# Decay rows of the delta net and mLSTM: spread over the partitions by DMA instead of by matmul

## The chip, the cores and the metric

The kernel runs on one core of a Trainium2 chip. The metric is the device time of one execution in microseconds (us). The engines are TensorE (PE; its weight loads are PEld), VectorE (DVE), ScalarE (ACT), GpSimd (POOL) and SyncE (SP), which only issues DMAs here. A transfer issued by SP or GpSimd runs on 16 DMA engines beside the compute engines.

## The reference

Two layers of a block for 256 latent and 256 context tokens of width 1024. Each layer modulates a layer norm, projects it into three token mixers (retention with 4 heads, mLSTM with 4 heads, gated delta net with 8 heads, each in both directions), gates and merges the branches, projects out, and ends with an MLP. In the second layer only the latent tokens are kept. All is float32. The two mixers that the change touches multiply their scores by decays:

```python
# delta net, per chunk
gc = jnp.cumsum(_chunks(g), axis=-1)
gdiff = gc[..., :, None] - gc[..., None, :]
decay = jnp.where(lower_incl, jnp.exp(jnp.where(lower_incl, gdiff, 0.0)), 0.0)
# mLSTM, per chunk
d_log = jnp.where(causal, b[..., :, None] - b[..., None, :] + ic[..., None, :], -jnp.inf)
w = jnp.exp(dl - m_i[..., None]) * jnp.einsum('bhid,bhjd->bhij', qq, kk)
```

In both, the exponent is a column (one number per key token) plus a row (one number per query token), masked to one triangle. The column is a per-partition bias. The row is the same on all 128 partitions, and so it has to be spread over them.

## The kernel before, in words

All 512 tokens stay on chip as feature-major tiles. A weight block of 1024 x 128 comes by one DMA into one of three `raw` buffers (`W`, L194), is split by ScalarE and VectorE into a high and a low part (`wh`, `wl`, three buffers each), and is used by 24 matmuls (`mm3`, L210). These projections are the stream on TensorE. The stages of the mixers are generators that a planner (`pump`, `stream`, L268 to L286) writes in between the steps of that stream: each step yields the time that it takes on TensorE and the time until its next step is ready. A scheduler then orders each engine's instructions from that program order and its own model of durations, and gives out the buffers; each engine and each DMA queue runs its list in order. A DMA can stand far ahead of its place in the program where its buffer is free.

The items of a layer are in the order `grgrgrgrgmgmgmgm`: `g` a delta-net head, `r` a retention head, `m` an mLSTM head. While one item is projected, stages of the two before it run.

The gate stage `small` (L534) computes all decays once per layer. Its results for the rows are put into one tile `rw` of 128 x 512: the delta net's 16 rows as a high part on partitions 0 to 15 and a rest on 32 to 47 (L597, L598), mLSTM's 8 rows on 64 to 71 and 96 to 103 (L639, L640). A constant `rows` selects one of them: `row(j)` (L643) is a column of it, broadcast to 128 x 128, and as stationary operand it makes TensorE sum the two parts of row j onto every partition.

A delta-net head (`gdn_mid`, L688) does for each direction: a bf16 product of the identity and the mask (0 or -1e30) into a PSUM tile `psch` of 512 columns, then the row's product on top of it (L743, L744). ScalarE takes the exponential of it with the column as bias, into a tile of the pool `s2` (three buffers). VectorE multiplies it with the scores, and at the end makes N. N goes to DRAM and to the inversion of small blocks on VectorE (`gdn_inv`), then to `gdn_merge`, whose mask products are on GpSimd, and to `gdn_chain`, whose PSUM tiles are the same two `psch` buffers.

An mLSTM head (`ml_scan`, L1000) makes its row once for each direction (L1021) and adds the mask to the diagonal tile with a bf16 product of 128 columns just ahead of the exponential (L1032, L1038). The pool `p` (16 buffers of 128 x 512) holds the projections of all items.

Of the kernel before, what the change touches and what calls it, by code (L numbers as in the profile page):

```python
# [8 lines left out]
F32 = mybir.dt.float32  # L9
F32R = mybir.dt.float32r  # L10
BF16 = mybir.dt.bfloat16
# [21 lines left out]
def shape_constants():  # L33
# [7 lines left out]
    b = np.zeros((128, 3, 128), f)  # L41
    b[:, 0] = np.eye(128)
    b[:, 1] = np.where(up > 0, 0.0, NEG)
    b[:, 2] = np.where(up.T > 0, 0.0, NEG)
    k['miscb'] = b.astype(ml_dtypes.bfloat16)
# [27 lines left out]
    rows = np.zeros((128, 24), f)  # L73
    for j in range(24):
        r = j if j < 16 else 48 + j
        rows[r, j] = rows[r + 32, j] = 1
    k['rows'] = rows
# [10 lines left out]
class Net:  # L88
    def __init__(self, ctx, tc, I, out, K):
# [9 lines left out]
    BUFS = dict(raw=3, wh=3, wl=3, ci=2, p=16, t=3, b=6, s1=5, s2=3, mg=8, v=3, my=2, vi=4,  # L99
                V=2, cR=2, cX=2, cXd=2, cS=4, sm=20)  # L100
# [38 lines left out]
    def consts(self):  # L139
        nc, K = self.nc, self.K  # L140
        m = self.T("kmisc", (128, 4, 128))
        nc.sync.dma_start(m, K['misc'])
        self.ident, self.tri_u, self.tri_l, self.ones = (m[:, j, :] for j in range(4))
        self.sel5 = self.T("ksel", (128, 8))
        nc.sync.dma_start(self.sel5, K['sel5'])
        self.sgn = self.T("ksgn", (128, 4))
        nc.sync.dma_start(self.sgn, K['sgn'])
        self.mhalf = self.sgn[:, 3:4]
        rw = self.T("krw", (128, 24))
        nc.sync.dma_start(rw, K['rows'])  # L150
        self.rows = self.T("krows", (128, 24), F32R)
        nc.scalar.copy(self.rows, rw)
        self.tri = [self.tri_u, self.tri_l]
        self.modc = {}
        self.early = 0

    def consts2(self):
        nc, K = self.nc, self.K
        mb = self.T("kmiscb", (128, 3, 128), BF16)
        nc.sync.dma_start(mb, K['miscb'])  # L160
        self.identb = mb[:, 0, :]
        self.negm = [mb[:, 1, :], mb[:, 2, :]]
# [3 lines left out]
        self.aident = self.T("kaid", (128, 128))  # L166
        self.ts(self.aident, self.ident, ALPHA)
# [13 lines left out]
    def rpow(self, out, in_, eps, n):  # L181
        """out = (in_ + eps) ** -0.5"""
# [11 lines left out]
    def W(self, ap, nk=8):  # L194
        """ap: DRAM [nk * 128, n] -> hi, lo [128, nk, n]"""
# [14 lines left out]
    def mm3(self, ps, w, xs, t0=0, n=L, clear=True):  # L210
        """generator: w^T x in ps, a step for each 128 of the contraction"""
# [38 lines left out]
    # Stages are generators. One that only streams projections yields the tensor engine's time in us; one with  # L250
    # products that wait for other engines yields (tensor engine's time, time until its next products are ready).
# [16 lines left out]
    def pump(self):  # L268
        """trace what is ready of the stages, the oldest first"""
# [28 lines left out]
    def cond(self):  # L298
        nc, I = self.nc, self.I
        cr = self.T("sc1", (16, 128))  # L300
# [20 lines left out]
    def ada(self, l, sec, half=None, exact=False, bank="mm", gap=0.0, tag="raw", after=None):  # L321
        """section sec of the conditioning as columns [128, 8, (x, ctx)]; exact: in float32 passes"""
# [41 lines left out]
    def feed(self, todo, gap):  # L364
        """sections of the conditioning one after the other, gap us between their steps"""
# [4 lines left out]
    def stats(self, src, n, eps=LN_EPS):  # L370
        """src [128, n*?]: mean and rstd over the free axis (chunks of <=512)"""
# [10 lines left out]
    def normed(self, src):  # L382
        """the layer norm of src [128, 1024], in place"""
# [11 lines left out]
    def ln_T(self, xn, pr):  # L395
        """normalised xn[t] [128,1024] of one segment -> modulated, feature-major, split: columns of h"""
# [33 lines left out]
    def post_half(self, uT, t, hf, last):  # L430
        """half the features of alpha * residual tile t + update, and their statistics"""
# [18 lines left out]
    def post_norm(self, ts, out, last=False):  # L450
        """new residual tiles t [128,1024], to out in DRAM, then in place their layer norm; step by step for all"""
# [35 lines left out]
    def norm_seg(self, uT, pr, hf, out, last=False):  # L487
        """residual update of a segment's two tiles, and the modulated norm of the result; half hf of the features"""
# [10 lines left out]
    def small_cols(self, l):  # L499
        nc, I = self.nc, self.I  # L500
        # column parameters
        cw = self.T("sc1", (120, 128))
# [5 lines left out]
        nw = self.T("sc1", (9, 128))  # L508
# [25 lines left out]
    def small(self, l, ps):  # L534
        nc, I = self.nc, self.I
        # per-row scalars
# [24 lines left out]
        self.ts(xs[q], xs[q], pr[q, 2:3])          # g rows 0..15, log_f rows 32..39  # L561
# [7 lines left out]
        # GDN: token-major g, beta  # L569
# [14 lines left out]
        # rows to be spread over the partitions: high parts from partition 0 and 64, the rest 32 further on  # L584
        rw = self.T("rw", (128, 512), F32R)
        nc.gpsimd.memset(rw.bitcast(F32), 0.0)
        z = self.T("gz", (128, 2, 4, 16))
# [9 lines left out]
        nc.scalar.copy(rw[0:16], pr_[0:16])  # L597
        self.tt(rw[32:48], pr_[0:16], rw[0:16].bitcast(F32), op=ALU.subtract)  # L598
        self.rw = rw
# [8 lines left out]
        # mLSTM rows 32..39  # L608
# [34 lines left out]
    def row(self, j):  # L643
        return self.rows[:, j:j + 1].to_broadcast([128, 128])

# [28 lines left out]
    def gtile(self, q=None):  # L674
        """a tile for the kept tokens: the unused half of q where there is one"""
# [4 lines left out]
    def silu2(self, ap, q):  # L680
        """2*silu(h @ ap), feature-major, for the tokens that are kept"""
# [6 lines left out]
    def gdn_mid(self, l, h, S):  # L688
# [4 lines left out]
        cs = lambda c: slice(c * 128, (c + 1) * 128)  # L693
        ss = self.T("ss", (128, 2, 4), bufs=2)
# [25 lines left out]
        bs = self.T("bs", (128, 2, 2, 4), bufs=3)    # [b | b*edl][dir][chunk]  # L720
# [20 lines left out]
        for d in range(2):  # L741
            rb = self.PS("ch").rearrange("p (c n) -> p c n", c=4)
            self.mm(rb, self.identb, self.negm[d].unsqueeze(1).to_broadcast([128, 4, 128]), start=True, stop=False)  # L743
            self.mm(rb, self.row(8 * d + h), self.rw.rearrange("p (c n) -> p c n", c=4), start=False)  # L744
            de = self.T("s2", (128, 4, 128))
# [9 lines left out]
            yield 2 * self.MM, 1.5  # L755
        # above the diagonal the forward system, below it the backward one
# [3 lines left out]
    def gdn_inv(self, l, h, S):  # L760
# [5 lines left out]
        # the forward systems' blocks on partitions 0..31, the backward ones', transposed, on 32..63  # L766
# [5 lines left out]
        # inverse of the unit upper-triangular blocks, last column first  # L772
# [19 lines left out]
    def gdn_merge(self, l, h, S):  # L792
        """from inverses of the 16-blocks to those of the 128-blocks, both directions in one matrix"""
# [4 lines left out]
        for lv in range(3):  # L798
# [3 lines left out]
            if lv < 2:  # L802
                # what the mask leaves of the transpose lies in the diagonal's blocks of 32
# [122 lines left out]
    def gate_out(self, b, k, ps, g, add1=False):  # L926
        """y^T tile k of branch b (without its constant factor) to DRAM"""
# [52 lines left out]
    def vtok(self, ap, ones=False):  # L980
        """token-major h @ ap for 256 columns: [128, token tile, 256 (+ a column of ones)]"""
# [18 lines left out]
    def ml_scan(self, l, h, S):  # L1000
# [4 lines left out]
        cs = lambda c: slice(c * 128, (c + 1) * 128)  # L1005
        ST = []
# [11 lines left out]
        for d in range(2):  # L1018
            dh = 4 * d + h
            nm = self.PS("ch")  # L1020
            self.mm(nm[:, t0:], self.row(16 + dh), self.rw[:, t0:])  # L1021
            yield 0.2, 0.3
            for seg in range(t0 // 256, 2):
                a, b = 2 * seg, 2 * seg + 1
                first, second = (a, b) if d == 0 else (b, a)
                # (key tile, query tiles it reaches) in scan order
# [3 lines left out]
                for n_, (j, it) in enumerate(js):  # L1030
                    if j // 2 == seg:
                        nc.tensor.matmul(nm[:, cs(j)], self.identb, self.negm[d], start=False, stop=True,  # L1032
                                         skip_group_check=True)
# [4 lines left out]
                    self.act(E, nm[:, r], AF.Exp, bias=self.atok[:, j, dh:dh + 1])  # L1038
# [19 lines left out]
    def head_ln(self, o, it):  # L1058
        """normalise every [128, 256] slice of o in place"""
# [28 lines left out]
    def rope(self, ps, ax, o, t0, scale):  # L1088
        """ps [128, 512 - t0] -> o (feature-major, rotated on the latent tokens)"""
# [324 lines left out]
```

## Time and profile before

| | |
|---|---|
| runs, us | 2602.63, 2602.08, 2606.39 (median 2602.63) |
| span of the profiled execution, us | 2602.6 |
| instructions | 42776 |
| busy: TensorE / its weight loads | 2524.0 us (97%) / 2143.0 us (82%) |
| busy: VectorE / ScalarE / GpSimd | 1754.2 us (67%) / 1305.3 us (50%) / 185.0 us (7%) |
| granted TensorE clock | 0.993 of full speed over the span |
| DMA | 337.92 MB, all of the kernel's own on SP's queue, 44.3% of 16 engines' time |

The span is that of the one execution that the profiler took, from its first to its last instruction, and that is the profiled execution's own time. Busy times count an engine as busy while one of its instructions runs. Matmuls are pipelined, so that the duration of one overlaps the next; the distance between the starts of neighbours tells what one costs. In a table of waits, A <- B means that A's engine stood still and that B ended it.

### The profile page before, as it was taken

Reading aid. Unit: us, or ns where it says so; the run is one execution under the profiler, and the core shown is the slowest. Engines: PE = TensorE matmul, PEld = TensorE weight load, DVE = VectorE, ACT = ScalarE, POOL = GpSimd, SP = SyncE. Lnnn points to the kernel's source line nnn. Section 1 sums busy time; section 2 is a strip of 40 time slices with the busy share of each in tenths; the row PEclk is TensorE's granted clock in tenths of the full one; section 3 lists DMA queues with packets and bytes.
Section 4 is the critical chain, followed back from the end, with each engine's and each line's share of the span. In section 5 each row is a group of like instructions: output and inputs, shape, how many; then the busy total and the mean of one; then the engine's idle time right before and its main releaser. Section 6 shows DMA issues by size and latency. Waiting matters only on the chain.

```text
span 2602.6 us, 42776 instructions
## 1 busy us (share of the span) xinstructions
PE 2524.0 (97%) x15265; PEld 2143.0 (82%) x15265; DVE 1754.2 (67%) x4692; ACT 1305.3 (50%) x3799; POOL 185.0 (7%) x347
## 2 busy tenths in 40 slices
PE   7999999999999999999999998899999999999998
PEld 3788888878887777787777786788888888997998
DVE  4876766676677455486455567887787777775666
ACT  3543544554455344366445446454535555554653
POOL 1000010010110000010000001011001100000000
PEclk9999999999999999999999999999999999999999
DMA  7323323312325555456555445333343334676764
GB/s 232 92 77 98 98 82 90 95 54 75 93 60 163 158 158 168 115 174 199 156 157 154 141 130 149 106 103 99 93 113 93 89 98 120 187 212 192 204 188 129
DMA packets 538023, 337.92 MB, mean 130 GB/s; under 512 B 46816, under 2 KB 502098, under 8 KB 537810
## 3 DMA queue, kind: packets, MB, share of 16 engines
q1 hardware_dynamic: 537810, 335.19, 44.3%
q8 instruction: 120, 1.97, 0.3%
q14 instruction: 93, 0.76, 0.1%
HBM read 314.17 MB, written 20.97 MB: 129 GB/s over the span
## 4 chain that ended last, share of the span: by engine, by line
PE 54%; DVE 8%; DMA 3%; ACT 2%; issue 1%; POOL 1%; SPq 0%; DVEq 0%; ACTq 0%; POOLq 0%
PE psmm L216 14%; PE psmm L220 14%; PE psmm L221 14%; PE psgr L136 3%; PE psch L136 2%; PE psmm L136 2%; PE pstr L136 2%; DVE p L130 1%; DVE wl L121 1%; PE pstr L133 1%; DMA my<-img 1%; DVE b L130 1%; POOL rs L121 1%; DMA xd<-b 0%; DVE s L130 0%
## 5 line engine op out<-in xcount | busy, mean ns | idle before, releaser
L191 ACT CAST wh<-raw 128x256 fp32r<-128x256 f32 (+1 forms) x1864 | 683.8, 420 | 735.5 <-PE psmm L220 521.9
L121 DVE TENSOR_TENSOR wl<-raw,wh 128x256 fp32r<-128x256 f32 (+1 forms) x1864 | 765.3, 447 | 325.8 <-ACT wh L191 322.2
L216 PE MATMUL psmm<-hh,wh 128*128 128x512 f32 (+1 forms) x2088 | 756.6, 363 | 18.6 <-ACT p L116 5.4
L220 PE MATMUL psmm<-hl,wh 128*128 128x512 f32 (+1 forms) x2088 | 730.7, 350 | 2.1 <-POOL hl L121 2.1
L221 PE MATMUL psmm<-hh,wl 128*128 128x512 f32 (+1 forms) x2088 | 726.1, 348 | 0.0
L216 PEld LDWEIGHTS psmm<-hh,wh 128*128 128x128 f32 x2088 | 394.8, 189 | 75.8 <-ACT p L116 6.3
L221 PEld LDWEIGHTS psmm<-hh,wl 128*128 128x128 f32 x2088 | 395.1, 189 | 53.1 <-DVE wl L121 0.9
L220 PEld LDWEIGHTS psmm<-hl,wh 128*128 128x128 f32 x2088 | 395.0, 189 | 50.7 <-POOL hl L121 3.3
L216 PE MATMUL psmm<-p,wh 128*128 128x256 f32 (+1 forms) x1152 | 368.4, 320 | 1.9 <-DVE mg L121 1.9
L220 PE MATMUL psmm<-p,wh 128*128 128x256 f32 (+1 forms) x1152 | 366.4, 318 | 0.6 <-DVE p L130 0.6
L221 PE MATMUL psmm<-p,wl 128*128 128x256 f32 (+1 forms) x1152 | 365.7, 318 | 0.4 <-DVE wl L121 0.4
L216 PEld LDWEIGHTS psmm<-p,wh 128*128 128x128 f32 x1152 | 216.9, 188 | 22.0 <-ACT sm L116 1.5
L220 PEld LDWEIGHTS psmm<-p,wh 128*128 128x128 f32 x1152 | 216.8, 188 | 18.0 <-DVE p L130 1.2
L221 PEld LDWEIGHTS psmm<-p,wl 128*128 128x128 f32 x1152 | 216.7, 188 | 17.0 <-DVE wl L121 0.9
L130 DVE SCALAR_TENSOR_TENSOR p<-ci,cw,p 128x512 f32<-128x512 f32 (+1 forms) x192 | 138.4, 721 | 9.4 <-ACT p L116 8.9
L136 PE MATMUL psmm<-wh,hh 128*128 128x256 f32 x512 | 143.6, 281 | 0.0
L136 PE MATMUL psmm<-wl,hh 128*128 128x256 f32 x512 | 143.3, 280 | 0.0
L136 PE MATMUL psmm<-wh,hl 128*128 128x256 f32 x512 | 143.2, 280 | 0.0
L136 PEld LDWEIGHTS pstr<-v,v 128*128 128x128 f32 x768 | 98.4, 191 | 11.5 <-issue 3.0
L136 PE MATMUL pstr<-v,v 128*128 128x128 f32 x768 | 103.3, 277 | 1.3 <-DVE hrs L125 0.4
L136 PEld LDWEIGHTS psmm<-wl,hh 128*128 128x128 f32 x512 | 96.2, 188 | 0.7
L136 PEld LDWEIGHTS psmm<-wh,hh 128*128 128x128 f32 x512 | 96.1, 188 | 0.7
(260 smaller groups left out, 3269.9 us busy)
## 6 DMA issues: line engine op xcount, KB each, us to landing
raw<-in_w_in_dram SPq DMA_DIRECT2D x224, 512.0 KB, 3.8
raw<-in_w_mlp_dram SPq DMA_DIRECT2D x136, 512.0 KB, 4.0
raw<-in_w_ada_dram SPq DMA_DIRECT2D x80, 512.0 KB, 3.6
raw<-in_w_branch_dram SPq DMA_DIRECT2D x48, 512.0 KB, 3.7
raw<-in_w_out_dram SPq DMA_DIRECT2D x24, 512.0 KB, 4.6
p<-in_w_ada_dram SPq DMA_DIRECT2D x32, 256.0 KB, 5.1
s<-const_toep_dram SPq DMA_DIRECT2D x40, 192.0 KB, 3.9
yd<-s SPq DMA_DIRECT2D x24, 256.0 KB, 2.3
```

The source lines that it names most:

```text
L121: (eng or self.nc.vector).tensor_tensor(out, a, b, op=op)
L130: self.nc.vector.scalar_tensor_tensor(out, a, s, b, op0=op0, op1=op1)
L133: self.nc.tensor.transpose(out, in_, ident if ident is not None else self.ident)
L136: self.nc.tensor.matmul(out, lhsT, rhs, start=start, stop=stop)
L191: self.nc.scalar.copy(hi, src)
L216: i = self.nc.tensor.matmul(ps, hi[:, k, :], a, start=(k == 0 and clear), stop=False, skip_group_check=not clear)
L220: self.nc.tensor.matmul(ps, hi[:, k, :], b, start=False, stop=False, skip_group_check=not clear)
L221: self.nc.tensor.matmul(ps, lo[:, k, :], a, start=False, stop=(k == 7), skip_group_check=not clear)
```

## The change

- `small` no longer makes `rw`. ScalarE copies the delta net's 16 rows into a tile of `p`, and two DMAs on SP's queue store 16 and 8 rows to DRAM (`grow`, `mrow`). The two subtractions that made the rests go.
- A new function `spread` brings a row to all partitions. For the delta net it loads a mask of 128 x 512 float32 from DRAM into a tile of a new pool `rb` (two buffers) with a DMA of SP, and then a DMA issued by GpSimd adds the row, read 128 times from DRAM, to it. For mLSTM it is one DMA of SP into a tile of `p`, without a mask.
- `gdn_mid` calls `spread` for both directions at its start, and takes the exponentials from that tile in place; `s2` and `psch` are not used there any more. Its steps yield no TensorE time to the planner.
- `ml_scan` adds the mask of a diagonal tile on VectorE, into the exponential's own tile; the first step of a segment takes two exponentials of 128 columns instead of one of 256. The second direction's row is loaded when the first is done, with 5 us for the planner.
- Constants: `rows`, its copy and the bf16 identity go; the scaled identity is made in the last layer, and some tiles share other pools (`sc1`, `gz` go; `sm` has 18 buffers instead of 20).

```diff
+    def spread(self, row, mask=None):
+        t = self.T("p" if mask is None else "rb")
+        if mask is None:
+            self.nc.sync.dma_start(t, row.partition_broadcast(128))
+        else:
+            self.nc.sync.dma_start(t, mask)
+            self.nc.gpsimd.dma_start(t, row.partition_broadcast(128), accum_op=ALU.add)
+        return t
...
-        nc.scalar.copy(rw[0:16], pr_[0:16])
-        self.tt(rw[32:48], pr_[0:16], rw[0:16].bitcast(F32), op=ALU.subtract)
-        self.rw = rw
+        gr = R()
+        nc.scalar.copy(gr[0:16], pr_[0:16])
+        nc.sync.dma_start(self.grow, gr[0:16])
...
-        nc.scalar.copy(rw[m2], u[m2])
-        self.tt(rw[96:104], u[m2], rw[m2].bitcast(F32), op=ALU.subtract)
+        nc.sync.dma_start(self.mrow, u[m2])
...
+        rbs = [self.spread(self.grow[8 * d + h, :], self.K['gmask'][d]) for d in range(2)]
...
-            rb = self.PS("ch").rearrange("p (c n) -> p c n", c=4)
-            self.mm(rb, self.identb, self.negm[d].unsqueeze(1).to_broadcast([128, 4, 128]), start=True, stop=False)
-            self.mm(rb, self.row(8 * d + h), self.rw.rearrange("p (c n) -> p c n", c=4), start=False)
-            de = self.T("s2", (128, 4, 128))
+            rb = rbs[d].rearrange("p (c n) -> p c n", c=4)
+            de = rb
...
-            yield 2 * self.MM, 1.5
+            yield 0.0, 1.5
...
+        nm = self.spread(self.mrow[h, :])
...
-            nm = self.PS("ch")
-            self.mm(nm[:, t0:], self.row(16 + dh), self.rw[:, t0:])
-            yield 0.2, 0.3
+            if d:
+                nm = self.spread(self.mrow[4 + h, :])
+                yield 0.0, 5.0
...
-                    if j // 2 == seg:
-                        nc.tensor.matmul(nm[:, cs(j)], self.identb, self.negm[d], start=False, stop=True,
-                                         skip_group_check=True)
...
-                    self.act(E, nm[:, r], AF.Exp, bias=self.atok[:, j, dh:dh + 1])
+                    at_ = self.atok[:, j, dh:dh + 1]
+                    if j // 2 == seg:
+                        for x, i in enumerate(it):
+                            Ex = E[:, x * 128:(x + 1) * 128]
+                            if i == j:
+                                self.tt(Ex, nm[:, cs(i)], self.negm[d], op=ALU.add)
+                                self.act(Ex, Ex, AF.Exp, bias=at_)
+                            else:
+                                self.act(Ex, nm[:, cs(i)], AF.Exp, bias=at_)
+                    else:
+                        self.act(E, nm[:, r], AF.Exp, bias=at_)
```

## Rows read from the trace of the kernel before

**Rows 1.** Page head and busy table: busy us (share of span) and instructions

```profile
span 2602.6 us, 42776 instructions
PE 2524.0 (97%) x15265; PEld 2143.0 (82%) x15265; DVE 1754.2 (67%) x4692; ACT 1305.3 (50%) x3799; POOL 185.0 (7%) x347
```

**Rows 2.** Stage table of two mixer stretches, by engine; columns in its first line

```profile
core 0: us, PE busy (x) PEld busy (x) DVE busy (x) ACT busy (x) POOL busy (x), PEclk, DMA share, GB/s
500.00:600.00 100.00, 98.40 (x571) 82.78 (x571) 69.36 (x211) 50.32 (x158) 8.41 (x16) 1.00 0.26 72
1880.00:2000.00 120.00, 115.44 (x762) 103.02 (x761) 90.17 (x270) 58.30 (x181) 10.62 (x25) 1.00 0.38 106
```

**Rows 3.** Timeline of TensorE, layer 0: start us, duration, engine, line, operation

```profile
395.06 0.39 PE L136 MATMUL psch<-kmiscb 128*128 128x512 bf16 x1
395.10 0.58 PE L136 MATMUL psch<-rw,krows 128*128 128x512 f32 x1
395.52 0.39 PE L216 MATMUL psmm<-hh,wh 128*128 128x512 f32 x1
395.75 0.40 PE L220 MATMUL psmm<-hl,wh 128*128 128x512 f32 x1
```

**Rows 4.** TensorE groups by shape: count, busy us, mean ns, idle before

```profile
L136 PE MATMUL psch<-rw,krows 128*128 128x512 f32 x40 | 21.7, 550 | 0.0
L136 PE MATMUL psch<-kmiscb 128*128 128x512 bf16 x32 | 12.2, 387 | 0.0
L1032 PE MATMUL psch<-kmiscb 128*128 128x128 bf16 x48 | 10.6, 221 | 0.0
L136 PE MATMUL psch<-rw,krows 128*128 128x256 f32 x8 | 3.0, 375 | 0.0
```

**Rows 5.** Timeline of TensorE at a mask of mLSTM, then in layer 1

```profile
618.71 0.22 PE L1032 MATMUL psch<-kmiscb 128*128 128x128 bf16 x1
618.73 0.47 PE L216 MATMUL psmm<-hh,wh 128*128 128x512 f32 x1
619.05 0.40 PE L220 MATMUL psmm<-hl,wh 128*128 128x512 f32 x1
...
2075.62 0.28 PE L216 MATMUL psmm<-hh,wh 128*128 128x256 f32 x1
2075.74 0.28 PE L220 MATMUL psmm<-hl,wh 128*128 128x256 f32 x1
```

**Rows 6.** Timeline of SP's queue, then VectorE, then ScalarE, around the first delta-net heads

```profile
65.02 0.32 SPq L503 DMA_DIRECT2D sc<-in_conv_w_dram  x1
...
208.16 0.69 DVE L121 TENSOR_TENSOR mg<-psgr,s 128x512 f32<-128x512 f32 x1
...
297.01 0.66 ACT L116 ACTIVATE s<-psch,gs 128x128 f32<-128x128 f32 x2
```

**Rows 7.** DMA issues by source and target: count, KB each, median us to landing

```profile
s<-const_toep_dram SPq DMA_DIRECT2D x40, 192.0 KB, 3.9
b<-in_ln_b_dram SPq DMA_DIRECT2D x4, 512.0 KB, 5.4
```

**Rows 8.** Users of PSUM tile psch: count, ns min/median/max, first and last start

```profile
L116 ACT ACTIVATE s<-psch,gs x128: 343/376/446, 105.7 to 2175.7; 128x128 f32<-128x128 f32 x128
L116 ACT ACTIVATE s<-psch,ae x80: 350/472/509, 525.1 to 2229.0; 128x256 f32<-128x256 f32 x56, 128x128 f32<-128x128 f32 x24
L121 DVE TENSOR_TENSOR mg<-psch,mg x80: 278/283/293, 173.9 to 2250.8; 128x128 f32<-128x128 f32 x80
```

**Rows 9.** Timeline of ScalarE at the start of layer 1

```profile
1635.90 0.57 ACT L597 CAST rw<-pstr 16x512 fp32r<-16x512 f32 x1 [1.92 <-PE pstr L136]
...
1647.10 0.37 ACT L116 ACTIVATE s<-psch,gs 128x128 f32<-128x128 f32 x1 [1.90 <-PE psch L136]
```

**Rows 10.** Who waited for whom: us in total, times, longest us

```profile
ACT s L116 <- PE psch L1032: 16.5, 16, 2.9
...
SPq L198 <- DVE wl L121: 1233.0, 344, 22.9
```

More of the change, by code (lines that the diff above doesn't have):

```diff
@@ L40, in shape_constants @@
     k['misc'] = np.ascontiguousarray(misc)
[L41 to L45, printed above, removed]
+    neg = [np.where(t > 0, 0.0, NEG).astype(f) for t in (up, up.T)]
+    k['negm'] = np.ascontiguousarray(np.stack(neg, 1)).astype(ml_dtypes.bfloat16)
+    k['gmask'] = np.ascontiguousarray(np.stack([np.tile(m, (1, 4)) for m in neg], 0))
     upm, lom = up > 0, up.T > 0
@@ L72, in shape_constants @@
     k['sel5'] = sel.reshape(128, 8)
[L73 to L77, printed above, removed]
     sg = np.zeros((128, 4), f)
@@ L99 @@
     BUFS = dict(raw=3, wh=3, wl=3, ci=2, p=16, t=3, b=6, s1=5, s2=3, mg=8, v=3, my=2, vi=4,
-                V=2, cR=2, cX=2, cXd=2, cS=4, sm=20)
+                V=2, cR=2, cX=2, cXd=2, cS=4, sm=18, rb=2)
     def T(self, tag, shape=(128, 512), dt=F32, bufs=None):
@@ L148, in consts @@
         self.mhalf = self.sgn[:, 3:4]
[L149 to L152, printed above, removed]
         self.tri = [self.tri_u, self.tri_l]
@@ L158, in consts2 @@
         nc, K = self.nc, self.K
[L159 to L162, printed above, removed]
+        mb = self.T("kmiscb", (128, 2, 128), BF16)
+        nc.sync.dma_start(mb, K['negm'])
+        self.negm = [mb[:, 0, :], mb[:, 1, :]]
         mk = self.T("kmmask", (128, 6, 128), BF16)
@@ L165, in consts2 @@
         self.mmask = mk
-        self.aident = self.T("kaid", (128, 128))
-        self.ts(self.aident, self.ident, ALPHA)
         zrow = self.T("p", (128, 512))
@@ L299, in cond @@
         nc, I = self.nc, self.I
-        cr = self.T("sc1", (16, 128))
+        cr = self.T("cR", (16, 128))
         nc.sync.dma_start(cr[0:8, :], I['c'].rearrange("o (k p) -> (o k) p", p=128))
@@ L500, in small_cols @@
         nc, I = self.nc, self.I
-        cw = self.T("sc1", (120, 128))
+        cw = self.T("jk", (120, 128))
         nc.sync.dma_start(cw, I['conv_w'][l].rearrange("t (k p) -> (t k) p", p=128))
@@ L507, in small_cols @@
         self.ts(self.cw, pw.rearrange("p (t k) -> p t k", t=5), 0.5)
-        nw = self.T("sc1", (9, 128))
+        nw = self.T("jk", (9, 128))
         nc.sync.dma_start(nw[0:8, :], I['mlstm_norm_w'][l].rearrange("(k p) -> k p", p=128))
@@ L583, in small @@
         yield 1.3, 0.3
-        rw = self.T("rw", (128, 512), F32R)
-        nc.gpsimd.memset(rw.bitcast(F32), 0.0)
-        z = self.T("gz", (128, 2, 4, 16))
+        self.grow = self.dr.tile([16, 512], F32, name=f"grow{l}", tag=f"grow{l}", bufs=1)
+        self.mrow = self.dr.tile([8, 512], F32, name=f"mrow{l}", tag=f"mrow{l}", bufs=1)
+        z = self.T("cX", (128, 2, 4, 16))
         nc.gpsimd.memset(z, 0.0)
@@ L638, in small @@
         self.ts(u[m2], Mf[m], -1.0)
-        nc.scalar.copy(rw[m2], u[m2])
-        self.tt(rw[96:104], u[m2], rw[m2].bitcast(F32), op=ALU.subtract)
+        nc.sync.dma_start(self.mrow, u[m2])
         yield 0.9, 0.0
-    def row(self, j):
-        return self.rows[:, j:j + 1].to_broadcast([128, 128])
+    def spread(self, row, mask=None):
[6 more added lines that the diff above has]
+        return t
     def gdn_proj(self, l, h, S):
@@ L1327, in begin @@
             def begin():
-                if not last:
+                if last:
+                    self.aident = self.T("cR", (128, 128))
+                    self.ts(self.aident, self.ident, ALPHA)
+                else:
                     self.drain(feed)
```

## The prediction

> **What bounds the kernel now.** I read the page's busy table first: TensorE is busy for 2524.0 of 2602.6 us and idle for 78.6 us [rows 1]. Two stretches of the mixers show the same by stage: in layer 0 TensorE is busy 98.40 of 100 us, in layer 1 115.44 of 120, while VectorE stands at 69.36 of 100 and 90.17 of 120, and GpSimd at about a tenth [rows 2]. A busy share can still hide slack, since matmuls overlap, so I went to the timeline. There the starts of two projection matmuls of 512 columns lie 395.75 - 395.52 = 0.23 us apart, back to back, with the products for the mask and the row pushed in between them [rows 3]. So in the mixers the time is what TensorE has to stream, and an instruction taken off it is worth the distance that it puts between its neighbours, not its recorded duration. The change is judged by that.
>
> **What leaves TensorE.** For a delta-net head and direction, the pair (mask product, row product) starts at 395.06 and the next projection matmul at 395.52: 0.46 us, twice the 0.23 us of a 512-column matmul [rows 3]. There are 32 such pairs (32 bf16 products of 512 columns) [rows 4]: 32 x 0.46 = 14.7 us. Of the 40 row products of 512 columns the other 8 are mLSTM's in layer 0: 8 x 0.23 = 1.8 us. In layer 1 mLSTM has 8 of 256 columns [rows 4]; two projection matmuls of that width start 0.12 us apart [rows 5]: 8 x 0.12 = 1.0 us. The 48 masks of 128 columns [rows 4] each delay the stream as follows: the projection matmul behind one starts at 618.73 and its successor at 619.05, a distance of 0.32 instead of 0.23; with the 0.02 us ahead of it that is 0.11 us [rows 5], 48 x 0.11 = 5.3 us. Sum off TensorE: 14.7 + 1.8 + 1.0 + 5.3 = 22.8 us, 12.7 of it in layer 0 (16 pairs 7.4, 1.8, 32 masks 3.5) and 10.1 in layer 1.
>
> **How much of it is kept.** In layer 0, where TensorE idles 1.6 of 100 us, I keep all but 1 us: 12. In layer 1 it idles 4.6 of 120 us and VectorE is at 75% [rows 2], so some of the work behind a removed product finds its operands late; I keep four fifths: 8. Together 20 us. The bounds are 22.8 (everything) and, if layer 1 is really paced by VectorE's weight splitting, 12.
>
> **The transfers of the delta net.** Each head gains two mask loads of 256 KB on SP's queue and two accumulating transfers of 256 KB on GpSimd's. Both need only a free buffer of the new pair (and the row in DRAM), and this program's order lets DMAs run far ahead: the second load of the convolution weights, written behind layer 0's output projection in the program, is issued at 65.02 us [rows 6]. The pair comes free when the head before has made its N, at 208.16 + 0.69 = 208.9 us, and the next head's first exponential is at 297.01 [rows 6]: 88 us of lead. The trace has no accumulating transfer and none issued by GpSimd; the nearest rows are 3.9 us for 192 KB and 5.4 us for a 512 KB broadcast of one DRAM row [rows 7]. I take 3.9 for the mask and 5.4 for the row; even twice the longer one for each, 22 us in all, fits into the lead. So I cost them at nothing; if the cover were gone, a head would wait 9 us. GpSimd issues in order: behind a transfer that waits for its mask stand the merge's mask products of the head before, the power behind the norms and the memsets of the convolution. In the stretch in which the transfers fall (right behind N, while VectorE inverts for some 30 us of plan) GpSimd has a tenth of work to do, so nothing urgent stands there. The exponentials then read SBUF instead of PSUM; both were 128 x 128 before at 376 ns from PSUM [rows 8], and I count no difference (bounds -0.1 to +0.1 us for each of 128, on an engine that is half idle).
>
> The first head of each layer has no lead: its rows come out of the gate stage. Layer 1 copies them at 1635.90 + 0.57 = 1636.5 and the first exponential runs at 1647.10 [rows 9]: 10.6 us for a small store to DRAM and the accumulating broadcast. With 3.9 for the store and 5.4 for the broadcast that is 9.3: just covered. Bounds for both layers together: -2 us (the row product used to wait for the mLSTM rows in the same tile, and no longer does) to +10. I take 0.
>
> **mLSTM.** Each diagonal tile gains a VectorE addition ahead of its exponential, and the first step of a segment has its exponential cut in two. The nearest addition of that size takes 283 ns [rows 8]: 48 x 0.283 = 13.6 us on VectorE, and 24 x 0.23 = 5.5 us more on ScalarE (two of 0.35, the least in the row, for one of 0.47 [rows 8]). Neither engine ends the wait most of the time; what reaches TensorE is the longer chain (addition, exponential, product) on the steps that are already late. On the other side, ScalarE waited 16.5 us in 16 places for the mask products in TensorE's queue [rows 10], and that wait goes. Bounds: -5 us, and +48 x 0.6 = +29 us if every step came late by the addition and a place in VectorE's queue. I take +3, near the lower end, since ScalarE's exponentials can run ahead of the products.
>
> SP gains 16 row loads of mLSTM into the pool `p`, which the projections use too. SP's queue mostly stands waiting for a weight buffer (1233.0 us in 344 waits, 3.6 us each [rows 10]); a row load that waits for a place in `p` holds the weight loads behind it. Three raw and three split buffers of 24 matmuls at 0.23 us are over 15 us of cover in layer 0. I take +1, with +16 x 3.6 = +58 us as the far bound.
>
> The rest: two small subtractions on VectorE go from each gate stage, constants move into other buffers, the scaled identity is made late: nothing that I can price. The planner gets other numbers (no TensorE time for the masks, 5 us for the second row), so neighbours move; I allow 5 us either way.
>
> **Sum.** 2602.6 - 20 + 0 + 3 + 1 - 1 (masks no longer occupy the two banks that the chain needs) = 2585.6. The span of the profiled execution, 2602.6, equals the median of the runs, 2602.63, so no correction is made. Forecast 2585 us, 0.7% less.
>
> **Rivals.** *A, the saving is eaten on the way* (chance 0.22). VectorE, at 75% in layer 1, paces more of it than I think, and the diagonal chain costs a quarter of its upper bound: -12 + 29 / 4 = -5, so 2598, between 2593 and 2603. For it: the waits of layer 1; against it: the back-to-back starts.
>
> *B, GpSimd's queue becomes the wait, and the kernel is slower* (0.12). The mask load may land later in real time than the order assumed, and GpSimd then stands in front of the merge's mask products. A hold of one mask landing, 3.9 us [rows 7], in 16 heads is 62 us at most; half of it reaching TensorE gives 2602.6 - 16 + 31 = 2618. It decides from 16/16 = 1.0 us per head. For it: order in the queue is fixed while landings vary. Against it: 88 us of lead and an engine nine tenths idle. The Trainium skill (SBUF — State Buffer, "SBUF: two separate sides") speaks for this rival: descriptors of a DMA issued from GpSimd are written by its cores, and a VectorE instruction in a two-port mode locks them out, with 620 ns growing to about 3100 ns in its example. As an estimate from that page, 32 transfers x 2.5 us = 79 us of extra hold, which on the path would give about 2660; no row of this trace shows such a transfer. The page also says ("Who interferes with whom") that tensor_tensor has no such mode, and VectorE's largest group here is of that kind, so I do not raise the chance for it.
>
> *C, more than TensorE's share* (0.08): with two PSUM banks for the chain and no de tile among the three `s2` buffers, part of the 78.6 us of idle goes too: 2602.6 - 23 - 8 = 2572.
>
> *D, the transfers do not land in time* in most heads (0.03): 9 us x 16 would be +144; the lead speaks against it.
>
> **Chances and range.** The forecast's own case, 2577 to 2593, holds 0.55. Two tenths of a percent, 5.2 us, is about what a measurement of this kernel can tell from no change. Faster by more (under 2597.4): 0.55 + 0.08 + half of A = 0.74; within: the rest of A and a little of B, 0.13; slower: the rest of B, and D, 0.13. The range goes from C's end to the upper end of A: 2573 to 2603.
>
> **What would show it.** Right: TensorE's instructions fall by 128, no product of mask or row is left, and its busy time falls by about 20 us while its idle time stays near 79. The accumulating transfers land tens of microseconds before the exponentials, except in the first heads. Wrong: ScalarE's exponentials wait for a DMA, GpSimd's merge products wait for a mask, SP stands before a row load, or TensorE's wait for mLSTM's weights grows beyond some 10 us. The forecast falls if TensorE's idle time grows by as much as its work shrinks.

## The result and the profile after

The changed kernel is slower: 2630.07 us, median of four runs (2627.53 to 2638.30), against 2603.53 us for four runs of the kernel before beside them. The ratio is 1.0105 [1.0091, 1.0120]. The prediction was 2585 us, and its range ended at 2603. The profiled execution of the changed kernel took 2629.87 us, and its span is 2628.1 us.

The head and the busy table of the page after, which answer to [rows 1]:

```profile
span 2628.1 us, 42743 instructions
PE 2510.1 (96%) x15137; PEld 2130.3 (81%) x15137; DVE 1757.5 (67%) x4736; ACT 1315.8 (50%) x3820; POOL 216.9 (8%) x377
```

TensorE lost exactly the 128 instructions (15265 - 15137), and its busy time fell by 13.9 us. But its idle time grew from 78.6 to 118.0 us, by 39.4 us. The difference of the two is the 25.5 us by which the span grew.

The stage tables tell where. The stages are the same in both kernels; each begins and ends at the same instruction of its trace. First before, then after (columns as in [rows 2]): three delta-net heads of layer 0, from N to N; then the rest of layer 0's mixers, with mLSTM; then the mixers of layer 1.

```profile
208.20:496.40 288.20, 288.20 (x1628) 245.53 (x1628) 206.19 (x570) 132.69 (x408) 25.41 (x47) 1.00 0.32 91
496.40:831.30 334.90, 330.26 (x1897) 275.24 (x1896) 230.53 (x680) 169.36 (x533) 32.81 (x61) 1.00 0.29 83
...
1654.90:2207.40 552.50, 533.53 (x3622) 481.75 (x3621) 425.51 (x1271) 283.49 (x885) 57.33 (x114) 1.00 0.37 103
```

```profile
206.90:503.30 296.40, 288.40 (x1609) 245.17 (x1608) 203.82 (x573) 132.44 (x407) 35.02 (x53) 0.99 0.36 97
503.30:846.90 343.60, 326.65 (x1866) 276.28 (x1865) 241.14 (x714) 181.69 (x561) 39.26 (x67) 0.99 0.37 101
...
1672.60:2240.60 568.00, 530.49 (x3566) 478.50 (x3564) 425.27 (x1278) 283.40 (x886) 69.44 (x128) 0.98 0.44 115
```

The three stages took 8.2, 8.7 and 15.5 us more: 32.4 us in the mixers, of which 7 us came back elsewhere. In the first stage TensorE had no idle time at all before, and has 8.0 us now. The third shows something that I had not looked for: the granted clock is 0.98 instead of 1.00, and TensorE's busy time fell by 3.0 us only, although the prediction takes 10.1 us of work off layer 1.

The waits of the changed kernel that have to do with the new transfers (us in total, times, longest; A <- B, as in [rows 10]):

```profile
ACT rb L110 <- DMA rb<-grow: 83.7, 24, 7.6
DVE vi L763 <- DMA vi<-nd: 47.0, 12, 7.9
POOL rb L636 <- DMA rb<-const_gmask_dram: 34.7, 16, 5.0
ACT s L110 <- DMA p<-mrow: 18.5, 7, 4.3
```

ScalarE waited 83.7 us for the delta net's rows, for which the prediction had read a lead of 88 us. The second line is an old wait, for N's transfer back from DRAM (the start of the inversion). Before it was this:

```profile
DVE vi L771 <- DMA vi<-nd: 30.6, 12, 5.7
```

One head shows how both come about. This is the timeline of the changed kernel right behind a head's N, which VectorE makes at 206.91: SP's queue, GpSimd, ScalarE, VectorE, TensorE.

```profile
206.68 0.33 SPq L635 DMA_DIRECT2D rb<-const_gmask_dram  x1
207.62 0.38 SPq L755 DMA_DIRECT2D nd<-mg  x1
208.04 0.50 SPq L185 DMA_DIRECT2D raw<-in_w_in_dram  x1
208.59 0.69 SPq L635 DMA_DIRECT2D rb<-const_gmask_dram  x1
210.62 0.33 SPq L760 DMA_DIRECT2D vi<-nd  x1
...
210.17 0.92 POOL L636 DMA_DIRECT2D rb<-grow  x1
...
216.59 1.28 ACT L110 ACTIVATE rb<-rb,gs 128x128 f32<-128x128 f32 x4 [7.63 <-DMA rb<-grow]
217.78 0.39 ACT L178 CAST wh<-raw 128x256 fp32r<-128x256 f32 x1
218.07 0.37 ACT L110 ACTIVATE p<-psmm 128x256 f32<-128x256 f32 x1
...
216.81 0.38 DVE L763 COPY vi<-vi 32x256 f32<-32x256 f32 x1 [4.50 <-DMA vi<-nd]
218.20 0.43 DVE L115 TENSOR_TENSOR wl<-raw,wh 128x256 fp32r<-128x256 f32 x1 [1.01 <-ACT wh L178]
...
219.96 0.41 DVE L124 SCALAR_TENSOR_TENSOR p<-psmm,b 128x256 f32<-128x256 f32 x1
...
302.54 1.28 DVE L115 TENSOR_TENSOR b<-psgr,rb 128x512 f32<-128x512 f32 x2
...
217.52 0.40 PE L208 MATMUL psmm<-hh,wl 128*128 128x512 f32 x1
220.52 0.36 PE L130 MATMUL psmm<-wh,hh 128*128 128x256 f32 x1 [2.60 <-DVE vi L772]
```

The accumulating transfer, issued at 210.17, lands 6.3 us later, at 216.5. The exponentials that read it belong to a head whose products with the scores, on VectorE, start at 302.54, 85 us later. But in ScalarE's queue they stand here, ahead of the split of the next weight block (217.78) and of the read-out of a finished projection (218.07), and ScalarE stands still for 7.63 us. Beside that, masks, N, its way back and a weight block are under way together, and VectorE waits 4.50 us for N's way back. TensorE stalls for 2.60 us. What ended that wait last, by the order of the rows, was a place for its results, and not weights (the row names the VectorE instruction that ended last before it): projections take turns in two `psmm` banks, and the one that its next products need holds a projection that VectorE finishes reading at 219.96 + 0.41 = 220.37, 0.15 us before TensorE goes on. The first piece of the next weight block was split by 218.20 + 0.43 = 218.63.

### The profile page after: what moved, and what is told of

It reads as the page before. It is cut to its first block, busy times and chain, and to the rows that moved or that the text cites. A ratio compares the mean times of both kernels' runs of the same rounds, so it can differ in the third digit from the quotient of the medians.

```text
span 2628.1 us, 42743 instructions
## 1 busy us (share of the span) xinstructions
PE 2510.1 (96%) x15137; PEld 2130.3 (81%) x15137; DVE 1757.5 (67%) x4736; ACT 1315.8 (50%) x3820; POOL 216.9 (8%) x377
## 5 line engine op out<-in xcount | busy, mean ns | idle before, releaser
L203 PE MATMUL psmm<-hh,wh 128*128 128x512 f32 (+1 forms) x2088 | 762.8, 366 | 26.5 <-DVE p L124 8.6
```

The lines of the kernel that those rows point to most:

```text
L203: i = self.nc.tensor.matmul(ps, hi[:, k, :], a, start=(k == 0 and clear), stop=False, skip_group_check=not clear)
```

## The experiments

Two suspects came out of the traces. The *early exponentials*: the program's order put the exponentials as far ahead as the transfers, because in the changed kernel they need nothing but the row's tile and the column. And the *pile-up*: the pair of buffers comes free at N, so the loads start in the same microseconds in which N goes to DRAM and comes back. A letter in an expectation names a theory within that text. Ratios are against the kernel before, run on the same chip.

**1. Hold the exponentials back** until the head's own `v` tiles are made.

```diff
-            self.act(vt[:, c, :], psv[:, c, :], AF.Copy, ...)
+            last_v = self.act(vt[:, c, :], psv[:, c, :], AF.Copy, ...)
...
+            with self.tc.issue_after(last_v.ins):
                 for c in kc:
                     self.act(de[:, c, :], rb[:, c, :], AF.Exp, ...)
```

> The changed kernel, with the delta net's row exponentials ordered on ScalarE behind the v tiles of their own head; every transfer stays. Theory: the loss is ScalarE standing before these exponentials, which were moved some 80 us ahead of their head to the moment at which the scheduler believed the row had landed (24 waits, 83.7 us in the changed kernel's trace). Then these waits fall under 5 us and the time comes back by 25 to 45 us, to 2585 to 2605. Rival 1, GpSimd's queue and the added transfers slow the kernel: the time stays within 2622 to 2635, since all of them are still there. Rival 2, the mLSTM part is the loss: it stays there too.

Measured: 2618.17 us, ratio 1.0056 [1.0036, 1.0076], between the theory (2585 to 2605) and the rivals (2622 to 2635). The wait of ScalarE for the row is gone from its trace, and 12 of the 26.5 us with it. The trace is that of the shortest of its four executions, 2609.63 us. The rest of the loss stays, and the wait for N's way back is as long as in the changed kernel. GpSimd stands before masks for longer (63.0 us, in the changed kernel 34.7), in a kernel that is faster. The last two lines, ScalarE's wait for mLSTM's rows and TensorE's for ScalarE's copies of mLSTM's scores, are for experiment 3:

```profile
POOL rb L636 <- DMA rb<-const_gmask_dram: 63.0, 14, 11.6
...
DVE vi L764 <- DMA vi<-nd: 47.0, 13, 7.5
...
ACT s L110 <- DMA p<-mrow: 26.3, 9, 5.8
...
PE pstr L130 <- ACT t L1008: 12.6, 9, 4.3
```

**2. How the cost goes with the number of transfers.** Both kernels have the hold. One adds a second accumulating transfer, of a row of zeros:

```diff
             self.nc.gpsimd.dma_start(t, row.partition_broadcast(128), accum_op=ALU.add)
+            self.nc.gpsimd.dma_start(t, self.K['zero'][0, :].partition_broadcast(128), accum_op=ALU.add)
```

> As the kernel with the exponentials held back, but each delta-net row has a second accumulating transfer behind the first, which adds a row of zeros: 32 more transfers of GpSimd. Theory: nobody waits for a transfer that lands tens of us ahead, so within 4 us of the kernel with one. Rival 1: GpSimd's queue or the transfers cost by number, so 32 more add what the first 32 did, 20 us or more.

The other has a single transfer for each tile, a broadcast by SP; masks, decay rows and GpSimd's transfers are left out (its decays are zero):

```diff
-            self.nc.sync.dma_start(t, mask)
-            self.nc.gpsimd.dma_start(t, row.partition_broadcast(128), accum_op=ALU.add)
+            self.nc.sync.dma_start(t, self.K['far'][0, :].partition_broadcast(128))
```

> As the kernel with the exponentials held back, but each of the delta net's 32 tiles is filled by a single broadcast DMA of SP from a constant row; the masks, the decay rows and GpSimd's transfers are left out, and the decays come out as zero. Two transfers for each tile gave 2618, three 2644. Rival 1 and the pile-up theory alike: one gives 2592 to 2606. If neither holds and the mLSTM half alone is what is left, 2612 to 2620.

Measured: three transfers 2644.07 us, 1.0166 [1.0148, 1.0185]; one 2604.54, 1.0000 [0.9986, 1.0014]. With the two of experiment 1 (1.0056) that is a row of 1, 2, 3 transfers: the second costs 0.56%, the third 1.10%. At this place transfers are not free, also without a consumer that waits early. The steps differ in more than the number, though. The single transfer also lacks the wait of the row for its mask. With three, GpSimd stands 118.2 us in 32 places until the first accumulating transfer has landed, while the wait for N's way back hardly grows (36.7, 47.0 and 47.9 us with one, two and three). What carries the third one's cost is open.

**3. The same transfers at another place.** Hold, and the rows go into the pool `v` of the merges, whose tiles come free behind the merge.

```diff
-        t = self.T("p" if mask is None else "rb")
+        t = self.T("p" if mask is None else "v")
```

> As the kernel with the exponentials held back (2618.2 us), but masks and rows go into buffers of the merge's pool v instead of a pool of their own. The same transfers then start when the merge of the head before is done, some 50 us later, instead of at the moment at which N is made. Theory, pile-up: next to N the mask, the row, N's way through DRAM and a weight block are under way together, and VectorE stands in order before N's blocks (DMA vi<-nd: 47.0 us against 30.6 in the kernel before) and before the retention tables; moved away from there, the time falls by 12 to 25 us to 2593 to 2606. Rival 1, the transfers and GpSimd cost by number wherever they stand: within 5 us of 2618.

Measured: 2598.68 us, ratio 0.9967 [0.9954, 0.9981]. Size, number and issuing engines of the transfers are the same as in experiment 1, and it is 0.9% faster, and faster than before. The stage tables of 2 us show the place itself. They begin some 5 us behind N: the hold alone, then hold and merge pool (the last but one figure is the mean busy share of the 16 DMA engines).

```profile
210.00:212.00 2.00, 2.00 (x11) 1.59 (x10) 0.97 (x3) 1.60 (x5) 0.00 (x0) 1.00 1.10 260
212.00:214.00 2.00, 2.00 (x10) 1.64 (x9) 0.90 (x2) 0.00 (x0) 0.00 (x0) 1.00 1.21 236
214.00:216.00 2.00, 1.87 (x9) 1.16 (x7) 1.11 (x4) 0.33 (x2) 0.00 (x0) 1.00 0.73 208
216.00:218.00 2.00, 1.03 (x9) 1.06 (x10) 1.97 (x9) 1.26 (x5) 0.58 (x1) 1.00 0.03 11
```

```profile
208.00:210.00 2.00, 2.00 (x11) 1.59 (x10) 0.97 (x3) 1.60 (x5) 0.00 (x0) 1.00 0.85 181
210.00:212.00 2.00, 2.00 (x10) 1.64 (x9) 1.27 (x4) 0.00 (x0) 0.00 (x0) 1.00 0.87 240
212.00:214.00 2.00, 2.00 (x11) 1.44 (x10) 1.91 (x8) 0.31 (x2) 0.00 (x0) 1.00 0.02 6
```

With the loads at N the DMA engines are full (1.10, 1.21) and busy for two microseconds longer, and TensorE loses 1.1 us there (1.87 and 1.03 of 2.00). With the loads elsewhere they are done by 212, and TensorE loses nothing. Over the kernel the wait for N's way back falls to half, and the two waits on mLSTM fall as well:

```profile
DVE vi L764 <- DMA vi<-nd: 23.7, 9, 4.8
...
ACT s L110 <- DMA p<-mrow: 17.4, 8, 4.4
...
PE pstr L130 <- ACT t L1008: 3.2, 3, 1.6
```

So the place costs 0.9%, but N's way back isn't shown to be all of it. From N to N, the three heads of layer 0 without mLSTM take 4.5 us less than with the hold alone, and those of layer 1 2.8 us more; the two stretches in which mLSTM heads run too take 8.4 and 7.5 us less. There TensorE waited less for ScalarE's copies of mLSTM's scores (the last line), which stand in ScalarE's queue with the exponentials that wait for mLSTM's rows. No run separates the two ways.

**4. The merge pool without the hold.** The edit is that of experiment 3 on the changed kernel:

```diff
-        t = self.T("p" if mask is None else "rb")
+        t = self.T("p" if mask is None else "v")
```

> The changed kernel with the delta net's masks and rows in the merge's pool of three buffers instead of their own pair, and without the hold on the exponentials. Theory H (two separate costs: exponentials put early into ScalarE's queue, about 12 us, and transfers piled up at N, about 19): only the second goes, about 2610, and ScalarE still waits tens of us for rows. Theory P (one cost: in the merge's pool the tile comes free only behind the merge, so the order has no early place for the exponentials either): 2596 to 2602, like the version with both, with no wait of ScalarE for a row.

Measured: 2630.79 us, ratio 1.0102 [1.0083, 1.0120]. Both theories missed: I had 2610 or 2599. The early exponentials alone cost as much as both together: with the merge pool the hold is worth 32 us, with the pair of buffers 12. The trace shows them mostly 4 to 6 us behind the accumulating transfers, at a new place. ScalarE, then TensorE in this kernel:

```profile
2118.62 0.40 ACT L110 ACTIVATE v<-v,gs 128x128 f32<-128x128 f32 x1 [4.83 <-DMA v<-grow]
...
2119.51 0.60 ACT L110 ACTIVATE cXd<-psch,bs 128x128 f32<-128x128 f32 x2
...
2119.91 1.23 PE L130 MATMUL psch<-cXd,mg 128*128 128x128 f32 x4 [4.99 <-ACT cXd L110]
```

The scaling `cXd` of the head in work stands behind the exponential of a later head, and TensorE, which needs it next, stalls 4.99 us for a wait of 4.83. In this kernel TensorE waited 21.6 us in 13 places for `cXd`; in the one of experiment 3 that wait is 1.5 us. So the two costs are not a sum. With the pair of buffers the wait of ScalarE fell together with the wait for N's way back, and part of it was paid already; I read the difference of 20 us that way, but no run separates it.

**5. mLSTM's half by itself.** First the changed kernel with the delta net as it was:

```diff
-            rb = rbs[d].rearrange("p (c n) -> p c n", c=4)
-            de = rb
+            rb = self.PS("ch").rearrange("p (c n) -> p c n", c=4)
+            self.mm(rb, self.identb, self.negm[d]...)
+            self.mm(rb, self.row(8 * d + h), self.rw...)
+            de = self.T("s2", (128, 4, 128))
```

> Only the mLSTM half of the change; the delta net's mask and rows are matmul products as before. Theory: near the kernel before, 2595 to 2606: 8 us of products go, some 18 us of ScalarE waits for the row of mLSTM come, of which a part reaches TensorE. Rival 2, the mLSTM half is the loss: 2618 or more.

Then the same without the row loads, a constant tile in their place (its decays are zero):

```diff
-            self.nc.sync.dma_start(t, row.partition_broadcast(128))
+        t = self.far
```

> mLSTM's half of the change alone (delta net as before), its rows replaced by a constant tile, so no load of a row; the additions on VectorE and the cut exponentials stay (its decays are zero). The half with its loads took 10.8 us more than before. Theory L (the loads, 16 through SP and the pool p): 2599 to 2605. Theory C (the longer chain and the changed plan): 2610 to 2616.

Then the kernel before with only the mask's addition moved to VectorE, the row still a product:

```diff
-                        nc.tensor.matmul(nm[:, cs(j)], self.identb, self.negm[d], ...)
...
+                                self.tt(Ex, nm[:, cs(i)], self.negm[d], op=ALU.add)
+                                self.act(Ex, Ex, AF.Exp, bias=at_)
```

> The kernel before, with one thing changed: mLSTM's mask is added on VectorE to the diagonal tile ahead of its exponential, as in the changed kernel; the row is still a matmul product. Theory A, the longer chain (addition, then exponential, then product) is what the mLSTM half costs: 2610 to 2616, like the mLSTM half alone (2614.5). Theory B, it is the wait for the row's transfer: 2596 to 2604, since 5.3 us of mask products go.

Measured: 2614.46 us, 1.0044 [1.0029, 1.0059]; 2609.27, 1.0016 [1.0004, 1.0027]; 2606.71, 1.0004 [0.9994, 1.0013]. Each lies between the two outcomes that were named for it. The 16 row loads cost 0.28%, 7 us, with some 5 us of doubt by the two intervals. The additions and the cut exponentials eat what the removed masks gave (1.0004) and, without the row loads, 4 us more than all removed products gave (1.0016). That the middle kernel, with fewer products than the last, is not faster stays unexplained; the planner's numbers differ between them too.

Then mLSTM's rows loaded earlier, into the same pool `p` (with the hold of experiment 1):

```diff
+        S["nm"] = [self.spread(self.mrow[h, :])]      # in ml_proj
...
-            if d:
-                nm = self.spread(self.mrow[4 + h, :])
+            nm = S["nm"][d]
```

> As the kernel with the exponentials held back, and mLSTM's two row loads are written earlier in the program: the first ahead of the projections of the head's gates, the second ahead of the first direction. Theory: the remaining waits of ScalarE for these rows (18.5 us in 7 places in the changed kernel) fall under 5 us, and the time falls by 3 to 10 us against the kernel with the exponentials held back. Rival: the second tile of the pool of projections held for longer makes projections wait, and the time rises by up to 10 us.

Measured: 2627.11 us, 1.0094 [1.0073, 1.0115], some 9 us more than with the hold alone, as the rival has it; that projections wait for the pool, the rival's reason, is not shown. The wait for N's way back is shorter (38.6 us) than in experiment 1, which is faster.

**6. The delta net's half with both cures**, mLSTM as before (hold and pool as in experiments 1 and 3, and this):

```diff
-        nm = self.spread(self.mrow[h, :])
...
+            nm = self.PS("ch")
+            self.mm(nm[:, t0:], self.row(dh), self.rw[:, t0:])
```

> The delta net's half of the change alone, with held exponentials and the buffers of pool v; mLSTM's rows and masks are matmul products as before. Theory: 14.7 us of products go, ScalarE stands before no row, nothing piles up next to N, and mLSTM's half, which cost 11 us alone, is not there: 2584 to 2595, below the kernel before (2603.6). Rival 1: 2605 or more.

Measured: 2600.16 us, 0.9984 [0.9972, 0.9996], faster than before, but between the theory (2584 to 2595) and the rival (2605). Next to a delta net that is cured, mLSTM's half costs nothing (0.9967 with it); next to the delta net of before it cost 11 us. The delta net's half as the change has it, without cures, wasn't run.

**7. All rows in the merge pool**, mLSTM's too, with the hold:

```diff
-        t = self.T("p" if mask is None else "v")
+        t = self.T("v")
```

> The version with hold and merge pool, with mLSTM's rows in the merge's pool too instead of p. Theory L (mLSTM's rows are issued late because they wait for a place in p; ScalarE waited 17 us in 8 places for them): 2588 to 2596, and those waits fall under 5 us. Rival: the pool of three is now shared by merges, masks and rows, a mask or a row waits there instead: 2600 to 2610.

Measured: 2592.36 us, ratio 0.9949 [0.9932, 0.9966], the best version. ScalarE's wait for mLSTM's rows falls from 17.4 us in 8 places (experiment 3) to 6.5 in 6, not quite under 5. Its mixers, to be held against the two tables at the top:

```profile
202.70:490.20 287.50, 287.33 (x1614) 245.01 (x1613) 206.22 (x572) 134.27 (x412) 33.52 (x53) 1.00 0.38 101
490.20:821.50 331.30, 323.84 (x1852) 272.94 (x1852) 232.52 (x708) 176.99 (x552) 38.52 (x65) 0.99 0.37 103
...
1653.80:2198.10 544.30, 522.62 (x3563) 474.48 (x3561) 423.60 (x1275) 285.41 (x884) 69.69 (x128) 0.99 0.46 119
```

**8. What the removed products are worth if no row is transferred at all**: the kernel of experiment 3, but its exponentials read one constant tile (decays are zero).

```diff
-        t = self.T("p" if mask is None else "v")
...
+        t = self.far if mask is None else self.T("v")
...
-            rb = rbs[d].rearrange("p (c n) -> p c n", c=4)
-            de = rb
+            rb = self.far.rearrange("p (c n) -> p c n", c=4)
+            de = rbs[d].rearrange("p (c n) -> p c n", c=4)
```

> The version with hold and merge pool, with no row and no mask transferred at all: the exponentials of the delta net and mLSTM read one constant tile (decays are zero). This is what the removed products are worth if transfers cost nothing. Theory S (the prediction's sum, of which the transfers still eat 14 us in the version with both): 2580 to 2586. Theory T (TensorE's saving of 19 us does not reach the end, whatever the transfers cost): 2593 to 2598, that is, within 5 us of the version with both, with TensorE idle for about 90 us instead of 79.

Measured: 2587.43 us, ratio 0.9933 [0.9919, 0.9948], just above the first theory (2580 to 2586), far from the second.

```profile
span 2583.3 us, 42569 instructions
...
PE 2499.3 (97%) x15137; PEld 2128.5 (82%) x15137; DVE 1761.6 (68%) x4736; ACT 1318.2 (51%) x3820; POOL 190.5 (7%) x346
```

## Why the prediction was wrong, step by step

**What leaves TensorE: right.** The sum was 22.8 us. With the transfers away TensorE's busy time is 2524.0 - 2499.3 = 24.7 us less. Its idle time is 84.0 us instead of 78.6, so 19.3 us of the span were kept (17.6 by the medians), where the prediction kept 20. Rival A, that VectorE's pace eats the saving, falls with this.

**The transfers of the delta net at nothing: the step that failed.** The transfers had the lead that I read: tens of microseconds before the head's products. I took the lead of the transfer for the lead of its consumer. [rows 6] shows where the exponentials ran when they stood behind a product of TensorE; that product held them there. With it gone, nothing in the program did, and the order moved them ahead along with the transfers, into the queue of an engine that works strictly in order. What late landing costs is then not "a head waits 9 us" but that whatever stands behind the exponentials waits: the weight split of the next block, the read-out of a projection, the scaling of the head in work. The trace shows the wait, 83.7 us in 24 places. Experiment 1 takes 12 us of the loss away by the order alone, experiments 3 and 4 differ by 32 us in nothing else. The Trainium skill states the base of it (PSUM — Partial Sum Buffer, "Engine vs sequencer instructions"): the queues of ScalarE, VectorE and GpSimd are strict FIFO. The trace agrees: the split at 217.78 follows the exponential, though its block was there. I had applied that to GpSimd's queue and not to ScalarE's.

**"Right behind N nothing urgent stands there": wrong too.** I looked at GpSimd's work in that stretch, a tenth, and not at the DMAs: N itself goes through DRAM there, and the inversion waits for it. The same transfers cost 0.9% more there than behind the merge (experiments 1 and 3), which is more than the whole predicted gain. The trace of before had the row for it, a wait of 30.6 us for N's way back, and I had not listed it among the waits that a new transfer could lengthen. 47.0 us is what it became. The place is shown by the runs; that N's way back carries the cost is argued from the rows at N. The length of that wait alone sets no price: it is 36.9 us in the third kernel of experiment 5, which has none of the new transfers and takes as long as the kernel before.

Together the two are more than the loss of 26.5 us: with both cures the kernel falls from 2630.07 us to 2598.68, by 31.4. Without transfers it is at 2587.43, and with mLSTM's rows moved too (2592.36) all but 5 us of that way is covered.

**mLSTM at +3, SP and `p` at +1: too small.** Next to the delta net of before this half takes 11 us more, of which 7 are the row loads (I had 1), inside the far bound of +58. The additions cost between 6 us (the masks' 5.3 us and the +1 of the third kernel of experiment 5) and 12 (the removed 8.1 and the +4 of the second), inside the bounds of -5 and +29. This term would have made the forecast 2585 + 11 + 8 - 4 = 2600, not slower than before.

**The first heads at 0: right.** At the start of layer 1 the rows are copied at 1653.74 + 0.58 and the first exponential runs at 1661.90, 7.6 us later; before it was 10.6 us [rows 9].

```profile
1653.74 0.58 ACT L585 COPY p<-pstr 16x512 f32<-16x512 f32 x1 [2.22 <-PE pstr L130]
...
1661.90 0.40 ACT L110 ACTIVATE rb<-rb,gs 128x128 f32<-128x128 f32 x1
```

**Rival B had the sign, but neither the size (2618) nor the place.** It put the wait on the merge's products behind GpSimd's transfers. GpSimd did stand 34.7 us before masks, but experiment 3 has those transfers on GpSimd's queue and is faster than before. Nor does SP's queue explain it: it stood before masks for 66 us in the changed kernel and for 144 us in experiment 3. The rule of the Trainium skill that spoke for it (SBUF — State Buffer, "SBUF: two separate sides", 620 ns that grow to about 3100) did not show: GpSimd's 32 transfers took 0.86 to 1.23 us each. Rival D, late landing in most heads, was priced as a wait of heads; the rows land 3.9 to 8.2 us after their issue, near the estimate of 5.4, and what waited for them was ScalarE's queue and not the heads.

What I said would show it wrong did so: ScalarE's exponentials wait for a DMA, and TensorE's idle time grew by more than its work shrank.

## What to carry to other kernels

A lead read from a trace belongs to an instruction and to what held it there: when a change removes the operand that tied a consumer to its place, ask where the order puts the consumer now, and what stands behind it in its engine's queue. Look at where the buffer of a new transfer comes free, because that is when the transfer starts, and at which DMA chain runs at that moment. Where both are put right, here with a hold and another pool, the change does give most of what the products cost: 2592.36 us instead of 2630.07, which is 12.7 us less than the kernel before beside it, of 17.6 without any transfer.

## What was not expected of the hardware

A stall can cost more than its length. In the changed kernel TensorE waited 2.3 us in a delta-net head of layer 0, and then ran at the lower clock (1.2 GHz, 0.50) for 3 us more. The stage table by microsecond:

```profile
316.00:317.00 1.00, 0.46 (x2) 0.02 (x1) 0.53 (x3) 1.00 (x5) 0.00 (x0) 1.00 0.99 157
317.00:318.00 1.00, 0.00 (x0) 0.00 (x0) 0.94 (x3) 0.63 (x3) 0.00 (x0) 1.00 0.10 16
318.00:319.00 1.00, 0.24 (x1) 0.27 (x2) 0.97 (x6) 1.00 (x4) 0.00 (x0) 0.85 0.00 0
319.00:320.00 1.00, 1.00 (x6) 1.00 (x7) 1.00 (x7) 1.00 (x4) 0.00 (x0) 0.50 0.00 0
...
321.00:322.00 1.00, 1.00 (x7) 1.00 (x6) 0.86 (x4) 0.00 (x0) 0.00 (x0) 0.50 0.34 52
...
324.00:325.00 1.00, 1.00 (x11) 1.00 (x10) 0.97 (x5) 0.00 (x0) 0.00 (x0) 1.00 0.00 0
```

At 0.50 it starts 6 or 7 matmuls of 256 columns in a microsecond, at 1.00 it starts 11: behind the stall of 2.3 us, 15 matmuls took 3.3 us (318.76 to 322.10), where 15 x 0.12 = 1.8 is what they cost at 1.00, so about 1.5 us more were lost. Time at the lower clock counts as busy time, and that fits a busy time that fell by 13.9 us only, with the work of 22.8 gone (with the same 15137 instructions it was 2499.3 us at a mean clock of 0.994 in experiment 8, and 2518.1 us at 0.986 with the three transfers of experiment 2). Over the span the mean granted clock was 0.988, before 0.993: (0.012 x 2628.1) - (0.007 x 2602.6) = 13 us more of clock not granted in these two executions; part of it fell into TensorE's idle time. It can't be read as a share of the loss: another execution of the changed kernel, with a mean clock of 0.992, took 2630.27 us, as long as this one. Not every stall has this after it; behind the one of 2.60 us that ended at 220.52 the clock stayed at 1.00.

A transfer that GpSimd issues holds GpSimd for 0.92 us and lands 5.7 us after its issue, at the median (256 KB, the row read 128 times). The Trainium skill says so of its kind (Perfetto Trace Analysis, "DMA Instruction — SWDGE (GPSIMD)"): the instruction's end in the profile is the end of writing descriptors and not of the movement. The rows agree as far as they go, since the instruction ends well before its transfer lands:

```profile
L636 POOL DMA_DIRECT2D rb<-grow x32: 856/915/1231, 93.3 to 2141.2; - x32
...
DMA to landing us min/median/max: 3.9/5.7/8.2
```
